# Attention head tiles in three pools, and the first head's three bias tables loaded during the query products

## The chip, the core and the metric

The kernel runs on one core of a Trainium2 chip. The core has a matrix engine (TensorE; PE in the profile, PEld for its weight loads), a vector engine (VectorE, DVE), a scalar engine (ScalarE, ACT), a general engine (GpSimd, POOL) and SyncE, whose queue SP issues all loads and stores of this kernel. Each engine takes its own instructions in order and waits where an operand or a buffer isn't ready. On-chip memory for data is one space in which the kernel opens and closes pools of equal slots; products land in PSUM banks. The metric is the time of one execution in microseconds (us); lower is better.

## What is computed

One layer of a trunk over 1024 latent tokens (a grid of 16 rows of 64) and 256 context tokens, width 1024, all in 32-bit floats:

```python
x = residual(x, swiglu(modnorm(x)))                   # half step
qa, ka, va, ... = project(modnorm(x))                 # one joint projection
o_na  = neighbourhood_attention(qa, ka, va, ...)      # 8 heads of 64
o_mla = blocked_attention(q_mla, k_mla, v_mla)        # 8 latent heads, 96 / 64
x = residual(x, merge(o_na, o_mla, gates))
x = residual(x, swiglu(modnorm(x)))                   # half step

# one grid row of the neighbourhood attention
s_loc = where(valid, q_r @ k_b + rpb[h, row_off, col_off], neg)
s_ctx = q_r @ k_ctx
p = softmax(concat(s_loc, s_ctx))
o = p_loc @ v_b + p_ctx @ v_ctx
```

A neighbourhood query sees a window of 8 by 16 grid cells with a relative bias, and all 256 context keys. Context tokens pass the first half step and the projection only.

## The kernel before

**Stages.** First half step; joint projection; latent, key and value products; query products of the latent attention (`q_heads`); then 64 attention items; merge; second half step. Up to the query products, work is laid out by `Plan`: a list of main steps with side steps spread beside them. Matrix products, turns (transposes on TensorE) and all loads and stores are kept in program order on their engines; the copies of the attention on VectorE and ScalarE may be ordered by the compiler.

**Products.** A 32-bit value is held as a high and a low part, so a product is two or three matrix instructions (`mm3`, `weigh`). All matrix instructions are issued at line 161 (`mmul`), turns at line 164 (`turn_`), loads and stores at line 132 (`put`). In tile names, `bs`, `bm` and `bv` are the three groups of PSUM banks, `w` the head tiles, `xy` tiles of pool y, `xf` of pool f, `t` half tiles, `xu` of pool u, `d` scratch in HBM, `in_bias` the tables.

**Heads and tiles.** A neighbourhood head h (`NaHead.loads`, line 1712) has these tiles, each loaded by SP:

- q and ql (queries, high and low), k (keys of the grid), kvc (context keys, later also context values): 512 KB each for the first three
- three bias tables of 384 KB; column block j uses table `BVAR[j]`, that is 0, 1, 1, 2
- va (values of blocks 0 and 1) and vb (blocks 2 and 3), 512 KB each

Loading is a generator with four steps: q, ql, kvc, k, table 0; table 1 and va; context values into kvc, and vb; table 2. All but table 2 are slots of 4 KB per partition in pool w, which has 13; table 2 lies in pool y with 2 slots. A latent head (`MlaHead`, line 2048) takes six slots of w: qh, ql, kh, kl, v, kvc. A slot may be loaded again once the last reader of the tile in it is done, and SP waits for that in its order.

**Items and rounds.** Item 4h + j of the neighbourhood heads is column block j of head h; items 32 to 63 are the latent heads. Round n of the loop at line 2215 works on the values of item n and starts the scores of item n + 3. A neighbourhood round has three parts (local, context, edge). In each part stand on TensorE, in this order: the turns of this part of item n; half of the scores of item n + 3 (two context and two local products for each half, in the first two parts); and a value product two parts old (`LAG`). So the context product of item n is issued in the first part of round n + 1, and its edge product in the second part. A local score is added to its bias table by VectorE at line 1983, the context score is copied at line 1954, line 1992 takes the exponent.

**When loads are issued.** `ahead_head` (line 2175) issues the first step of head h in the third part of round 4(h-1). `na_item` (line 2136) issues the other steps when item 4h is started, in round 4h - 3. Before the loop, side steps beside the second half of the query products (line 1903) issue three steps of head 0 and the first of head 1, and score items 0 and 1, whose probabilities lie in pool f (`EARLY` = 2). Head 0's table 2 is issued when item 2 is started, in round 0, since pool y opens only after the query products, in memory that pools u and t leave.

**Memory.** On the left side, w (13 slots) and f (2 of 5 KB) lie where pool v was. On the right side, after the query products: o (16), y (2), t (12 of 2 KB), u (10).

Of the kernel before, what the change touches and what calls it, by code (L numbers as in the profile page):

```python
# [8 lines left out]
F32 = mybir.dt.float32  # L9
F32R = mybir.dt.float32r  # L10
# [5 lines left out]
P = 128  # L16
# [22 lines left out]
def f32(ap):  # L39
    return ap.bitcast(F32)  # L40
# [3 lines left out]
def hybrid_block(ctx: ExitStack, tc: tile.TileContext, a: dict, out: bass.AP):  # L44
# [9 lines left out]
    pools = {}  # L54

    def nm(s):
        count[0] += 1
        return f"{s}_{count[0]}"

    def open_pool(key, name, bufs, side):  # L60
        pools[key] = tc.alloc_tile_pool(name=nm(name), bufs=bufs, side=side, reuse_waits="tile")

    def close_pools(*keys):
        for key in keys:
            pools.pop(key).release()

    def U(dt=F32, key="u"):
        return pools[key].tile([P, 1024], dt, tag="u", name=nm("x" + key))
# [1 line left out]
    def V(dt=F32):  # L70
        return U(dt, "v")

    def W(dt=F32R):
        return pools["w"].tile([P, 1024], dt, tag="w", name=nm("w"))

    def T2(dt=F32, n=512):
        return pools["t"].tile([P, n], dt, tag="t", name=nm("t"))
# [34 lines left out]
    class Engine:  # L112


        def __init__(self, e):
            self.e = e
# [5 lines left out]
    def ld(dst, src):  # L122
        for x in [x for x in waiting if x[1].tensor.name == src.tensor.name]:
            waiting.remove(x)
            put(*x[1:])
        return put(dst, src)
# [4 lines left out]
    def put(dst, src):  # L131
        return pin(nc.sync.dma_start(dst, src))
# [987 lines left out]
    class Raw:  # L1120

        us = {(name, hl): [U(F32R, "v") for _ in range(2)] for name in ("a11", "a12") for hl in range(2)}
        f = {}
# [95 lines left out]
    plan = Plan()  # L1219
# [23 lines left out]
    o = len(plan.main)  # L1243
# [64 lines left out]
    o = len(plan.main)  # L1308
# [12 lines left out]
    o, tail = down1.plan(plan)  # L1321
# [110 lines left out]
    def emit_lat(d, ci, x, bank):  # L1432
        t, sq = T2() if bank else x, T2()

        def high():
            if bank:
                act.copy(t, x)
            store(cqT[d][:, ci * 512:(ci + 1) * 512], t)
            act.activation(sq, t, AF.Square)
            later(add, 1)  # L1440

        def add():
            if ci in squares:
                vec.tensor_tensor(squares[ci], squares[ci], sq, op=ALU.add)
            else:
                squares[ci] = sq
        later(high)

    for p in range(3):
        punits.append(Unit(h2, [wc_cols(2 * p), wc_cols(2 * p + 1)],  # L1450
                           lambda i, ci, x, bank, p=p: emit_lat(2 * p + i, ci, x, bank)))
# [21 lines left out]
    o = len(plan.main)  # L1473
# [67 lines left out]
    class Set:  # L1541
# [16 lines left out]
        def loads(self):  # L1558

            return [lambda j=j: self.load(j) for j in range(2)]  # L1560
# [50 lines left out]
    o = len(plan.main)  # L1611
# [97 lines left out]
    class NaHead:  # L1709


        def loads(self, h):
            self.h = h
            i, b = h // 2, (h % 2) * 64
            self.q, self.ql, self.kvc, self.k = q, ql, kvc, k = [W() for _ in range(4)]
            for s in range(2):
                o = 64 * s
                ld(f32(q[o:o + 64, :]), qas[i][0, b:b + 64, :])
                ld(f32(ql[o:o + 64, :]), qas[i][1, b:b + 64, :])
                ld(f32(kvc[o:o + 64, 0:256]), kas[i][s, b:b + 64, NLAT:])  # L1720
            for s in range(2):
                ld(f32(k[64 * s:64 * s + 64, :]), kas[i][s, b:b + 64, :NLAT])
            self.bias = [W(F32)]
            ld(self.bias[0][:, :768], a["bias"][h, 0])
            yield
            self.bias.append(W(F32))
            ld(self.bias[1][:, :768], a["bias"][h, 1])
            self.va = va = W()
            for j in range(2):
                self.values(va, j)  # L1730
            yield
            ld(f32(kvc[:, 256:512]), vcs[h])
            self.vb = vb = W()
            for j in range(2, 4):
                self.values(vb, j)
            yield
            self.bias.append(U(F32, "y"))
            ld(self.bias[2][:, :768], a["bias"][h, 2])
            yield

        def values(self, v, j):
# [3 lines left out]
    def na_loads(h):  # L1745
        heads["na", h] = x = NaHead()
        yield from x.loads(h)
# [97 lines left out]
    o = va_at  # L1845
# [9 lines left out]
    o = len(plan.main)  # L1855
# [4 lines left out]
    o = len(plan.main)  # L1860
# [3 lines left out]
    o = len(plan.main)  # L1864
# [3 lines left out]
    o = len(plan.main)  # L1868
    plan.step(*calls(q_heads(1, cqn[1]), 9))
    heads = {}  # L1870
    EARLY, AHEAD = 2, 3
# [3 lines left out]
    def na_next(h, n=1):  # L1875
        if h not in na_open:
            na_open[h] = na_loads(h)
        for _ in range(n):
            next(na_open[h], None)

    def weights():
        close_pools("v")
        open_pool("w", "weights", 13, "left")
        open_pool("f", "first", EARLY, "left")

    def score_banks():
        banks[0] = "mv"
# [3 lines left out]
    def first_scores(j):  # L1891
        if len(early) == j:
            it = na_item(0, j)
            started.append(it)
            early.append(it.scores())
        next(early[j], None)
# [3 lines left out]
            soft.pop(0)()  # L1900

    plan.spread([weights], o - 4, o - 3)
    plan.spread([lambda h=h: na_next(h) for h in (0, 0, 0, 1)], o - 3, o + 5)
    plan.spread([score_banks], o + 2, o + 3)
    plan.spread([lambda j=j: first_scores(j) for j in (0, 0, 1, 1)], o + 4, o + 8)
    plan.spread([first_soft] * 2, o + 6, o + 9)
# [141 lines left out]
    class MlaHead:  # L2048
        def __init__(self, h):
            self.h = h  # L2050
            self.qh, self.ql, self.kh, self.kl, self.v, self.kvc = [W() for _ in range(6)]
            b, i = (h % 2) * 64, (h % 4) * 32
            for s, x in enumerate((self.qh, self.ql)):
                ld(f32(x[0:64, :]), qns[h // 2][s, b:b + 64, :])
                ld(f32(x[64:QK, :]), qrs[h // 4][s, i:i + 32, :])
                ld(f32(self.kvc[0:64, s * 256:(s + 1) * 256]), kns[h // 2][s, b:b + 64, NLAT:])
                ld(f32(self.kvc[64:QK, s * 256:(s + 1) * 256]), krs[s, :, NLAT:])
            for s, x in enumerate((self.kh, self.kl)):
                ld(f32(x[0:64, :]), kns[h // 2][s, b:b + 64, :NLAT])
                ld(f32(x[64:QK, :]), krs[s, :, :NLAT])  # L2060
            vsv = vs[:, h * P:(h + 1) * P].rearrange("(t p) c -> p t c", p=P)
            ld(f32(self.v).rearrange("p (t c) -> p t c", t=8), vsv[:, 0:8, :])
            ld(f32(self.kvc[:, 512:768]).rearrange("p (t c) -> p t c", t=2), vsv[:, 8:10, :])
# [70 lines left out]
    soft, started = [], []  # L2134
    edges = []
    def na_item(h, j):
        if (j == 0) if h else (j == EARLY):
            na_next(h, 4)
        return NaItem(heads["na", h], j)

# [5 lines left out]
    def items_():  # L2146
        for h in range(NH):
            for j in range(4):
                yield lambda h=h, j=j: na_item(h, j)
        for h in range(NH):  # L2150
            for b in range(4):
                yield lambda h=h, b=b: mla_item(h, b)
# [6 lines left out]

    close_pools("u", "t")  # L2160
    open_pool("o", "heads", 16, "right")
    open_pool("y", "third", 2, "right")
    open_pool("t", "half", 12, "right")
    open_pool("u", "units", 10, "right")
    for x in (ona, omla):
# [9 lines left out]
    def ahead_head(h):  # L2175
        if h < NH:
            na_next(h) if h > 1 else None
        else:
            heads["mla", h - NH] = MlaHead(h - NH)

    def start(n):

        if n < len(todo):
            it = todo[n]()
            started.append(it)
            yield from it.scores()
# [28 lines left out]
    for n in range(len(todo)):  # L2215
        ahead = chain(*[start(x) for x in (range(EARLY, AHEAD + 1) if n == 0 else (n + AHEAD,))])
        for d in range(2):
            if n == len(todo) - 6 + d:
                fm.load(d)
            if n == len(todo) - 5 + d:  # L2220
                fm.split(d)
        parts = started[n].values()
        soft_n, soft[:] = list(soft), []
        for x, part in enumerate(parts):
            pending.append(part())
            for _ in range(-(-len(soft_n) // (len(parts) - x))):
                soft_n.pop(0)()
            for _ in range(5 // len(parts)):
                next(ahead, None)
            if n % 4 == 0 and x == 2 and n // 4 + 1 < 2 * NH:  # L2230
                ahead_head(n // 4 + 1)
            if n >= len(todo) - 3 and (n, x) != (len(todo) - 3, 0) and len(fm.todo) > 4:
                fm.step()
            if len(pending) > LAG:
                pending.pop(0)()
        for _ in ahead:
            pass
    for w in pending:
        w()
        fm.step()  # L2240
# [1 line left out]
        fm.step()  # L2242
    pinned[0] = False

    close_pools("u", "t", "y", "f", "w")
    open_pool("t", "half", TBUFS, "left")
    open_pool("u", "units", 24, "left")

# [35 lines left out]
    plan = Plan()  # L2284
# [5 lines left out]
    for d in range(KD):  # L2290
        o = len(plan.main)
# [21 lines left out]
    plan = Plan()  # L2313
# [30 lines left out]
    o = len(plan.main)  # L2344
# [13 lines left out]
    o = len(plan.main)  # L2358
# [14 lines left out]
    o, tail = down2.plan(plan)  # L2373
# [108 lines left out]
```

## Time and profile before

| | us |
|---|---|
| median of 3 runs | 2557.65 |
| lowest, highest | 2557.51, 2558.33 |
| the profiled execution | 2555.57 |
| its span in the trace | 2553.8 |

Times in the profile are in us from the start of the span. The page lists the busy time of each engine; a view of waits says which engine's instruction ended the idle time of another; a timeline lists instructions in order of time, equal neighbours merged: start, duration, engine, line, operation, output and inputs, shape, count, and in brackets the idle time before it with what ended it. SPq rows are the issue of loads and stores, not their transfer; the time from issue to landing stands in the view of DMA issues. The last columns of the windows' view give the granted clock of TensorE, the busy share of the DMA engines and what they moved in GB/s.

The query products run up to about 1333, the neighbourhood items from there to about 1475, the latent items to about 1742.

### The profile page before, as it was taken

The numbers are of one execution on the slowest core, as the hardware profiler recorded it, in microseconds if no ns is written. First come the engines' busy times: TensorE is split into PE (matmuls) and PEld (weight loads), VectorE is DVE, ScalarE is ACT, GpSimd is POOL, SyncE is SP. The second block draws the span as 40 slices with busy tenths as digits, with TensorE's granted clock in tenths as the row PEclk, the third lists the DMA queues.
The fourth block names the chain that finished last, engine by engine and source line by source line (L and its number), as shares of the span: only waits on it lengthen the run. The fifth ranks groups of instructions, "written<-read, shape, count | busy, mean of one in ns | idle before, by whom it ended". The sixth has DMA issues, their size and how long they took to land.

```text
span 2553.8 us, 38179 instructions
## 1 busy us (share of the span) xinstructions
PE 2526.1 (99%) x13007; PEld 2145.5 (84%) x13007; DVE 1897.7 (74%) x3627; ACT 1249.9 (49%) x2389; POOL 242.5 (9%) x425
## 2 busy tenths in 40 slices
PE   8999999999999999999999999999999999999998
PEld 6888888888888788889889999988888888888887
DVE  5788887898567687874559988886445888777557
ACT  6623223555346753333439888782355322233633
POOL 1000000000002100001007622220030000000001
PEclk9999999999999999999999999999999999999999
DMA  8477765779576665766899832215135667556755
GB/s 315 162 242 236 242 225 189 274 246 297 180 239 221 241 220 190 229 225 200 286 287 243 224 78 77 77 32 210 67 131 179 212 222 236 183 185 251 248 203 193
DMA packets 275475, 523.32 MB, mean 205 GB/s; under 512 B 33424, under 2 KB 84432, under 8 KB 275280
## 3 DMA queue, kind: packets, MB, share of 16 engines
q1 hardware_dynamic: 275280, 520.88, 61.6%
q8 instruction: 103, 1.69, 0.3%
q14 instruction: 92, 0.75, 0.1%
HBM read 375.47 MB, written 145.29 MB: 204 GB/s over the span
## 4 chain that ended last, share of the span: by engine, by line
PE 86%; ACT 6%; DVE 5%; issue 2%; POOL 0%; DMA 0%; DVEq 0%; POOLq 0%; ACTq 0%
PE bs L161 33%; PE bm L161 30%; PE bv L161 20%; ACT xu L2091 2%; PE bm L164 2%; DVE xu L1954 1%; PE bs L164 1%; ACT t L2117 1%; DVE t L2118 1%; DVE xv L120 1%; ACT xu L1992 1%; ACT t L2091 0%; ACT t L1926 0%; ACT t L120 0%; PE bv L164 0%
## 5 line engine op out<-in xcount | busy, mean ns | idle before, releaser
L120 ACT CAST xu<-t 128x512 fp32r<-128x512 f32 x589 | 346.8, 621 | 673.3 <-DVE t L120 558.1
L161 PE MATMUL bm<-xu,xu 128*128 128x512 f32 (+1 forms) x2442 | 596.0, 388 | 0.9 <-ACT t L120 0.9
L161 PEld LDWEIGHTS bm<-xu,xu 128*128 128x128 f32 x2442 | 450.1, 188 | 92.1 <-ACT t L120 2.0
L120 DVE TENSOR_TENSOR xu<-t,xu 128x512 fp32r<-128x512 f32 x589 | 383.0, 688 | 77.5 <-ACT xu L120 77.1
L161 PE MATMUL bs<-xu,xu 128*128 128x512 f32 (+2 forms) x1581 | 388.3, 384 | 0.0
L161 PE MATMUL bs<-xv,xu 128*128 128x512 f32 x1512 | 363.5, 389 | 0.2 <-DVE t L120 0.2
L161 PEld LDWEIGHTS bs<-xu,xu 128*128 128x128 f32 x1581 | 291.7, 188 | 58.0
L161 PE MATMUL bv<-xv,xu 128*128 128x512 f32 x1342 | 336.0, 389 | 0.0
L161 PEld LDWEIGHTS bs<-xv,xu 128*128 128x128 f32 x1512 | 283.5, 188 | 59.7 <-issue 1.0
L161 PEld LDWEIGHTS bv<-xv,xu 128*128 128x128 f32 x1342 | 251.6, 188 | 52.1
L120 DVE TENSOR_TENSOR xu<-xu,xu 128x512 fp32r<-128x512 f32 x282 | 190.0, 689 | 64.4 <-ACT xu L120 63.4
L120 DVE TENSOR_TENSOR t<-t,t 128x512 f32<-128x512 f32 (+4 forms) x350 | 221.2, 635 | 13.5 <-ACT t L120 8.8
L161 PE MATMUL bs<-w,w 96*128 96x512 f32 (+3 forms) x832 | 206.0, 365 | 5.4 <-DVE st L1983 5.4
L161 PE MATMUL bv<-xu,xu 128*128 128x512 f32 x722 | 191.5, 389 | 0.0
L120 POOL TENSOR_SCALAR st<-st 128x1 f32<-128x1 f32 x60 | 27.1, 452 | 1630.9 <-ACT t L120 1283.6
L120 ACT CAST xu<-xu 128x512 fp32r<-128x512 f32 x282 | 169.5, 621 | 11.3 <-DMA xu<-in_f1w 8.0
L161 PEld LDWEIGHTS bv<-xu,xu 128*128 128x128 f32 x722 | 135.5, 188 | 28.1
L161 PE MATMUL bm<-t,xu 128*128 128x256 f32 (+1 forms) x920 | 156.9, 332 | 0.0
L161 PEld LDWEIGHTS bm<-t,xu 128*128 128x128 f32 x920 | 137.4, 189 | 18.6
L161 PE MATMUL bv<-t,w 128*128 128x256 f32 x896 | 150.7, 288 | 1.9 <-DVE t L2118 1.4
L161 PEld LDWEIGHTS bv<-t,w 128*128 128x128 f32 x896 | 133.1, 190 | 17.5 <-DVE t L2118 6.0
L161 PEld LDWEIGHTS bs<-w,w 96*128 96x128 f32 (+1 forms) x832 | 123.2, 190 | 14.2 <-DVE st L1983 7.7
(231 smaller groups left out, 3192.6 us busy)
## 6 DMA issues: line engine op xcount, KB each, us to landing
d<-t SPq DMA_DIRECT2D x432, 256.0 KB, 2.9
t<-d SPq DMA_DIRECT2D x348, 256.0 KB, 5.0
xu<-in_f1w SPq DMA_DIRECT2D x104, 512.0 KB, 4.4
xu<-in_f2w SPq DMA_DIRECT2D x58, 512.0 KB, 4.7
t<-in_wada SPq DMA_DIRECT2D x112, 256.0 KB, 4.5
w<-d SPq DMA_DIRECT2D x112, 256.0 KB, 5.0
t<-in_f1w SPq DMA_DIRECT2D x77, 256.0 KB, 5.0
t<-in_f2w SPq DMA_DIRECT2D x77, 256.0 KB, 5.2
```

The lines of the kernel that those rows point to most:

```text
L120: return lambda *x, **y: pin(f(*x, **y))
L161: return pin(nc.tensor.matmul(o, s, m, start=start, stop=stop, skip_group_check=open_group[0]))
L164: return pin(nc.tensor.transpose(o, x, i))
L1954: nc.vector.tensor_scalar(dst, src, 1.0, FMIN, op0=ALU.mult, op1=ALU.max, accum_out=m)
L1992: soft.append(lambda s=s: nc.scalar.activation(pr[s][:, :640], pr[s][:, :640], AF.Exp, bias=n_[:, s:s + 1], accum_out=l[:, s:s + 1]))
L2091: nc.scalar.activation(x, x, AF.Exp, bias=n_[:, s:s + 1], accum_out=l[:, i:i + 1])
L2117: nc.scalar.copy(t[0], pb)
L2118: nc.vector.tensor_tensor(t[1], pb, f32(t[0]), op=ALU.subtract)
```

## The change

Head tiles are spread over more pools. Pool w falls from 13 slots to 8. The tables go into a pool y of 4 slots of 3 KB per partition, now on the left side and opened with w, before the query products end. For odd neighbourhood heads, kvc and k lie in a new pool p of 2 slots, opened on the right after the query products where y was. Pool f gets a third slot, which no item uses; after round 1 it is closed, and a pool x of 3 slots opens in its place. A latent head takes four slots of w (qh, ql, kh, kl), its kvc from x, and its v from p (the first one's from x).

Beside the query products all four steps of head 0 are now issued, table 2 among them; the first step of head 1 is issued when pool p is open, before the loop.

```diff
-    def W(dt=F32R):
-        return pools["w"].tile([P, 1024], dt, tag="w", name=nm("w"))
+    def W(dt=F32R, key="w", n=1024):
+        return pools[key].tile([P, n], dt, tag=key, name=nm(key))
...
-            self.q, self.ql, self.kvc, self.k = q, ql, kvc, k = [W() for _ in range(4)]
+            self.q, self.ql = q, ql = W(), W()
+            self.kvc, self.k = kvc, k = [W(key="p" if h % 2 else "w") for _ in range(2)]
...
-            self.bias = [W(F32)]
-            ld(self.bias[0][:, :768], a["bias"][h, 0])
-            yield
-            self.bias.append(W(F32))
-            ld(self.bias[1][:, :768], a["bias"][h, 1])
+            self.bias = []
+            for j in range(2):
+                self.bias.append(W(F32, "y", 768))
+                ld(self.bias[j], a["bias"][h, j])
+                if j == 0:
+                    yield
...
-            self.bias.append(U(F32, "y"))
-            ld(self.bias[2][:, :768], a["bias"][h, 2])
+            self.bias.append(W(F32, "y", 768))
+            ld(self.bias[2], a["bias"][h, 2])
...
-        open_pool("w", "weights", 13, "left")
-        open_pool("f", "first", EARLY, "left")
+        open_pool("w", "weights", 8, "left")
+        open_pool("y", "third", 4, "left")
+        open_pool("f", "first", 3, "left")
...
-    plan.spread([lambda h=h: na_next(h) for h in (0, 0, 0, 1)], o - 3, o + 5)
+    plan.spread([lambda: na_next(0)] * 4, o - 3, o + 5)
...
-            self.qh, self.ql, self.kh, self.kl, self.v, self.kvc = [W() for _ in range(6)]
+            self.qh, self.ql, self.kh, self.kl = [W() for _ in range(4)]
+            self.kvc = W(key="x")
...
+            self.v = W(key="p" if h else "x")
...
-        if (j == 0) if h else (j == EARLY):
+        if h and j == 0:
             na_next(h, 4)
...
     open_pool("o", "heads", 16, "right")
-    open_pool("y", "third", 2, "right")
+    open_pool("p", "parts", 2, "right")
+    na_next(1)
...
+        if n == EARLY - 1:
+            close_pools("f")
+            open_pool("x", "parts", 3, "left")
...
-    close_pools("u", "t", "y", "f", "w")
+    close_pools("u", "t", "p", "x", "y", "w")
```

## The prediction

> **What bounds the kernel now.** The page's table of engines comes first: the sum of busy time says how much any change can win.
>
> ```profile
> span 2553.8 us, 38179 instructions
> PE 2526.1 (99%) x13007; PEld 2145.5 (84%) x13007; DVE 1897.7 (74%) x3627; ACT 1249.9 (49%) x2389; POOL 242.5 (9%) x425
> ```
>
> TensorE idles for 2553.8 - 2526.1 = 27.7 us of the whole span. Its list of waits says how much of that lies in the stage that the change touches, the neighbourhood attention:
>
> ```profile
> PE bs L161 <- DVE st L1983: 5.4, 7, 1.9
> ```
>
> Seven waits, 5.4 us, for the instruction that adds the bias table (L1983). The two long ones stand at the start of that stage, in the timeline of TensorE:
>
> ```profile
> 1337.42 1.11 PE L161 MATMUL bs<-w,w 128*128 128x256 f32 x4 [1.39 <-DVE st L1983]
> 1341.92 1.10 PE L161 MATMUL bs<-w,w 128*128 128x256 f32 x4 [1.88 <-DVE st L1983]
> ```
>
> So 1.39 + 1.88 = 3.3 us go there, and about 2.1 us in the other five. That is all the change can win. What it can lose depends on when each head's loads may start, and that is read from the queue SP, which issues every load. Rows of its timeline, in several stretches:
>
> ```profile
> 1334.82 0.32 SPq L132 DMA_DIRECT2D d<-t  x1
> 1335.23 0.41 SPq L132 DMA_DIRECT2D xy<-in_bias  x1
> 1340.83 9.26 SPq L132 DMA_DIRECT2D w<-d  x8
> 1345.17 1.08 SPq L132 DMA_DIRECT2D w<-d  x2
> 1349.00 1.09 SPq L132 DMA_DIRECT2D w<-d  x2
> 1355.12 0.33 SPq L132 DMA_DIRECT2D w<-in_bias  x1
> 1355.97 2.22 SPq L132 DMA_DIRECT2D w<-d  x5
> 1371.69 2.44 SPq L132 DMA_DIRECT2D w<-d  x5
> ```
>
> The eight w<-d at 1340.83 are head 2's q, ql, kvc, k. They stop twice: kvc at 1345.17, k at 1349.00. Each stop ends as another tile of pool w has its last reader:
>
> ```profile
> 1344.57 0.56 DVE L1983 CUSTOM_DVE_ANT_0 xu<-bs,w 128x384 f32<-128x384 f32 x1
> 1345.06 0.08 DVE L1983 DVE_READ_ACCUMULATOR2_ANT st<- 128x1 f32 x1
> ```
>
> ```profile
> 1348.31 0.65 PE L161 MATMUL bv<-xu,w 128*128 128x256 f32 x4
> 1354.45 0.64 PE L161 MATMUL bv<-t,w 128*128 128x256 f32 x4
> 1354.93 0.60 PE L164 MATMUL bm<-ident,xu 128*128 128x128 f32 x4
> 1355.28 0.84 PE L161 MATMUL bs<-w,w 128*128 128x256 f32 x4
> 1355.96 0.64 PE L161 MATMUL bv<-xu,w 128*128 128x256 f32 x4
> 1357.49 0.84 PE L161 MATMUL bs<-w,w 128*128 128x256 f32 x4
> 1371.00 0.84 PE L161 MATMUL bs<-w,w 128*128 128x256 f32 x4
> 1373.39 0.48 PE L161 MATMUL bs<-w,w 128*128 128x256 f32 x2
> ```
>
> kvc goes out at 1345.17, after head 1's first bias table was last read (1345.14); k at 1349.00, after item 1's edge product (1348.96), the last reader of head 0's va; head 2's second table at 1355.12, after item 3's context product (1355.09), the last reader of head 0's kvc. A load takes the slot that comes free next, within 0.05 us, and everything behind it on SP waits too. That queue is the thing to count. Now it keeps ahead: k of head 2 is issued at 1349.00 and first needed by item 8's scores at 1357.49.
>
> **The change, part by part.**
>
> *First head's tables.* Table 2 of head 0 (issued at 1335.23) moves into the query products, and head 1's first step (q, ql, kvc, k, table 0) moves out of them to the front of the attention, since its kvc and k now lie in pool p, opened there. The query products lose 2 MB of loads. TensorE is busy throughout there (columns of the windows' view: stretch, its length, busy time of TensorE and its count, and so on), so I count nothing.
>
> ```profile
> 1310.00:1320.00 10.00, 10.00 (x61) 8.92 (x60) 5.77 (x22) 1.58 (x3) 0.00 (x0) 1.00 1.07 257
> 1320.00:1330.00 10.00, 10.00 (x53) 8.45 (x52) 5.43 (x15) 5.27 (x9) 0.90 (x2) 1.00 0.74 232
> ```
>
> Head 1's nine loads then start at 1335.23, behind the same last store (1334.82). Their pace: the five of 1355.97 take about 0.45 us each, those with the short kvc rows, by the first row below, about 0.62 us.
>
> ```profile
> 1345.66 1.87 SPq L132 DMA_DIRECT2D w<-d  x3
> ```
>
> I take 0.55 us. From issue to landing, asked for loads issued at 1346 to 1347, at 1349.3 to 1350 (an emptier queue), and at 1361.6 to 1362 (a full one):
>
> ```profile
> w<-d SPq DMA_DIRECT2D x2, 256.0 KB, 4.5
> w<-d SPq DMA_DIRECT2D x2, 256.0 KB, 3.9
> w<-d SPq DMA_DIRECT2D x1, 256.0 KB, 7.4
> ```
>
> I take 5.0 us for the last of a batch of seven, with 3.5 and 7.0 as ends; here 5.5, since stores are still in flight. The eighth load, the second half of k, is issued at 1335.23 + 7 x 0.55 = 1339.1 and lands at 1344.6. Item 4's local scores, which read it, begin now some 0.35 us after 1341.92, at 1342.3. **+2.3 us** (0 to 4). The waits of 3.3 us removed before that point buy nothing: TensorE reaches the same missing k earlier.
>
> *Slots of the later heads.* With tables gone, an even head takes 6 slots of w, an odd one 4. Two consecutive heads need 10, and there are 8. For **even heads** (2, 4, 6): when head 2's q, ql, kvc, k are wanted, head 1 holds 4 slots (q, ql, va, vb) until item 7's last scores, and all that head 0 had must be empty but two. q and ql find slots early; kvc must wait for head 0's kvc, that is item 3's context product, ending at 1355.09; k follows with a slot freed by item 7's scores at about 1356.1, which costs nothing more as SP gets there later. The rest of the step stands behind kvc: kvc, q, ql, kvc, k, k, table. The sixth is issued at 1355.09 + 5 x 0.55 = 1357.8 and lands at 1362.8. Item 8's local scores begin now at about 1357.49 + 0.34 = 1357.8. TensorE takes its instructions in order, so the products, turns and later scores queued behind stand too, and with them VectorE and ScalarE. **5.0 us** each (with 0.47 and 3.5: 3.1; with 0.64 and 7.0: 7.5).
>
> For **odd heads** (3, 5, 7): q and ql come from w, kvc and k from p. Head 2 holds 6 slots, head 1 its va and vb: 8, none free. q gets head 1's va after item 5; ql must wait for head 2's q, ql or k, that is item 11's last scores, about 1371.7 (SP's row at 1371.69 now starts on that event), or for head 1's vb, later still. Behind ql stand kvc, q, ql, kvc, k, k: the second k is the seventh, issued at 1371.7 + 6 x 0.55 = 1375.0, landed at 1380.0. Item 12's local scores are due at about 1373.8. **6.2 us** (4.2 to 8.7).
>
> Each wait is measured from an event on TensorE, so one stall does not shorten the next. Three of each: 15.0 + 18.6 = **33.6 us** (21.9 to 48.6). The tables no longer hold SP: with 4 slots in y, each slot was last read before SP comes to it.
>
> *The latent heads.* Their first head needs kl in a slot freed by item 31's last scores, one round before use; kh, kl and kl's second half are issued within some 1.7 us of item 27's context product and land near 6 us after it. The scores that read them come some 4.4 us after it, by the rows of item 3 (1355.09 to item 8's scores at 1357.49, then 2 us of context scores, products and turns). **+1.5 us** (0 to 3). Later ones have longer rounds, 32 of them between the last edge product at 1475.2 and 1741.6, so 8.3 us each, and two whole sets of four slots: nothing.
>
> ```profile
> L161 PE MATMUL bv<-xu,w x128: 276/282/385, 1344.4 to 1475.2; 128*128 128x256 f32 x128
> 1739.38 2.23 PE L161 MATMUL bm<-xo,w 128*128 128x512 f32 x9
> ```
>
> *Pools x and f, and the end.* x opens on memory whose readers ended 26 rounds earlier. At the end the residual branch's loads already wait in the kernel before, and go on waiting for the same two last tiles: nothing, give or take 1 us.
>
> *Gains kept.* The five small waits at the heads' seams, 2.1 us, are covered by the longer ones: **-1.5 us** (-2.1 to 0).
>
> Sum: 2.3 + 33.6 + 1.5 - 1.5 = **+35.9 us**, from +20.3 to +55.6 by the ends. The profiled execution took 2555.57 us (its span and 1.8 us round it), so 2591.5 there; the median of the runs shown is 2557.65, 2.1 us above, so I forecast 2593.5.
>
> **The rivals.**
>
> *Half speed after each stall.* Before its first work TensorE idles for 8.86 us; then the same turns take longer than 4 us later:
>
> ```profile
> 9.52 0.42 PE L164 MATMUL bm<-ident,xv 128*128 128x128 f32 x1
> 11.84 0.42 PE L164 MATMUL bm<-ident,xv 128*128 128x128 f32 x1
> 14.04 0.27 PE L164 MATMUL bm<-ident,xv 128*128 128x128 f32 x1
> ```
>
> They are slow from 8.86 to past 11.84, for some 3.3 us. If a stall of 5 to 6 us brings the same back, at 0.27/0.42 of the pace, each costs 1.2 us more: six of them 7 us, about 2600.5. Against it: the longest idle later is 1.88 us, and no slow turn follows it, so the length from which it decides is not shown. [...]
>
> *The loads arrive in time, and the kernel is faster.* If slots are handed out so that kvc and ql come free a round earlier, or if a whole step lands within the 2.7 us between item 3's context product and item 8's scores, nothing stalls; then the 3.3 us at the start and the 2.1 us at the seams are won: 2557.65 - 5.4 = 2552.2. For it: the fastest load of pool w took 1.9 us. Against it: six loads need 2.8 us for their issue alone, and the count of slots leaves no other order.
>
> ```profile
> DMA to landing us min/median/max: 1.9/4.2/8.8
> ```
>
> *Only the first heads feel it.* SP's blocking could be less than I think if the even heads' kvc found an early slot: then +2.3 us and the seams' gain cancel, 2558. The same time comes out if the change only shuffles idle of the queue.
>
> **How the numbers follow.** Stalls at six heads, full speed: 0.62, at 2593.5. Half speed besides: 0.22, at 2600.5. In time and faster: 0.07, at 2552. No difference: 0.09, at 2558. The first two hold 0.84; their range runs from a little under the low end of the sum (2578) to near its high end (2613): 2575 to 2612, which leaves the other two out. A measurement of this kernel can tell about 0.2%, 5.1 us, from no change. Slower 0.84, faster 0.07, within 0.09.
>
> **What would show it.** Right: from 1340 us on TensorE's bs<-w,w stands idle for 4 to 8 us once a head, ended by a load of w, seven times; SP's w<-d rows of even heads start just after a bv<-t,w product, those of odd heads after the last bs<-w,w; the heads come every 21 to 22 us in place of 15.9 (1357.49 to 1373.39); the query products and the latent heads keep their length; TensorE's idle grows from 27.7 to above 55 us at the same busy time. Wrong: SP's loads of a head issued more than 9 us before its first scores, or stalls ended by L1983 rather than a load.

## The result, and the profile after

| | us |
|---|---|
| before, median of 4 runs | 2557.75 |
| after, median of 4 runs | 2614.69 (2612.52 to 2617.75) |
| ratio | 1.0223, interval 1.0210 to 1.0235 |
| profiled execution, before and after | 2555.57 and 2612.52 |

The change costs 57 us. It was forecast to be slower, by 36 us; the time lies 2.7 us above the range. The table of engines of the changed kernel divides the loss:

```profile
span 2610.7 us, 38181 instructions
PE 2543.0 (97%) x13007; PEld 2161.6 (83%) x13007; DVE 1899.5 (73%) x3627; ACT 1247.7 (48%) x2389; POOL 241.8 (9%) x425
```

TensorE's idle time grew from 27.7 to 2610.7 - 2543.0 = 67.7 us, by 40.0. Its busy time grew too, by 2543.0 - 2526.1 = 16.9 us, for the same 13007 instructions. The two sum to 56.9 us, the whole difference of the profiled executions (56.95).

**The idle part.** The list of waits of TensorE (engine, what it waited for, total us, times, longest) has two new rows, loads of tiles in p and w, and the old row of bias additions (now at line 1986) is down from 5.4 to 1.4 us:

```profile
PE bs L161 <- DMA p<-d: 25.4, 8, 5.6
PE bs L161 <- DMA w<-d: 16.9, 8, 3.7
PE bs L161 <- DVE st L1986: 1.4, 1, 1.4
```

In the timeline of TensorE head 2 looks so:

```profile
1361.13 0.64 PE L161 MATMUL bv<-t,w 128*128 128x256 f32 x4
...
1363.82 0.60 PE L164 MATMUL bm<-ident,xu 128*128 128x128 f32 x4
1367.78 0.48 PE L161 MATMUL bs<-w,w 128*128 128x256 f32 x2 [3.36 <-DMA w<-d]
1369.86 0.98 PE L161 MATMUL bs<-w,w 128*128 128x384 f32 x2 [1.60 <-DMA w<-d]
1370.63 1.05 PE L161 MATMUL bv<-t,p 128*128 128x256 f32 x4
1371.49 1.05 PE L164 MATMUL bm<-ident,xu 128*128 128x128 f32 x4
...
1375.93 0.60 PE L164 MATMUL bm<-ident,xu 128*128 128x128 f32 x4
```

and the same stretch on SP:

```profile
1355.67 0.45 SPq L132 DMA_DIRECT2D w<-d  x1
...
1361.80 1.72 SPq L132 DMA_DIRECT2D w<-d  x3
1362.94 2.50 SPq L132 DMA_DIRECT2D w<-d  x4
```

The last two rows sum up two neighbouring stretches and overlap. The context product of item 3 ends at 1361.77 (1361.13 + 0.64); SP, which has issued nothing since the ql of 1355.67, issues kvc at 1361.80 and then the rest of the step. Item 8's context scores wait 3.36 us for q and kvc, its local scores 1.60 us more for k: 4.96 us. Odd heads, here head 3, wait longer:

```profile
1393.21 0.77 PE L161 MATMUL bs<-p,w 128*128 128x256 f32 x2 [5.34 <-DMA p<-d]
1395.46 0.98 PE L161 MATMUL bs<-p,w 128*128 128x384 f32 x2 [1.48 <-DMA p<-d]
```

**The busy part.** Look at the turns of head 2 above: four take 1.05 us after the wait and 0.60 us from 1375.93 on. The windows' view (the column after POOL's is the granted clock) shows why: TensorE's granted clock is 0.50 there.

```profile
1365.63:1369.04 3.41, 0.48 (x2) 0.31 (x2) 0.37 (x1) 1.20 (x4) 2.52 (x6) 1.00 1.04 217
1369.04:1375.86 6.82, 6.00 (x26) 6.03 (x27) 2.42 (x9) 1.49 (x4) 0.00 (x0) 0.50 0.89 328
1375.86:1379.28 3.42, 3.42 (x29) 3.42 (x29) 3.00 (x10) 3.23 (x8) 2.18 (x4) 1.00 0.00 0
```

The same view puts one window of 20 us round each of the seven waits; the first and the last:

```profile
1340.00:1360.00 20.00, 15.01 (x100) 14.60 (x100) 11.80 (x44) 12.22 (x30) 8.70 (x21) 0.83 0.71 204
...
1485.00:1505.00 20.00, 14.49 (x98) 14.26 (x99) 11.68 (x40) 11.18 (x29) 8.98 (x17) 0.83 0.79 222
```

All seven show a mean clock of 0.83. With a clock of 0.50, as at head 2, the missing 0.17 x 20 = 3.4 us are 6.8 us of half speed each time. Part of it still falls into the wait, and 16.9 / 7 = 2.4 us are lost on work.

### The profile page after: what moved, and what is told of

Its sections match the earlier page's. It is cut to its first block, busy times and chain, and to the rows that moved or that the text cites. A ratio compares the mean times of both kernels' runs of the same rounds, so it can differ in the third digit from the quotient of the medians.

```text
span 2610.7 us, 38181 instructions
## 1 busy us (share of the span) xinstructions
PE 2543.0 (97%) x13007; PEld 2161.6 (83%) x13007; DVE 1899.5 (73%) x3627; ACT 1247.7 (48%) x2389; POOL 241.8 (9%) x425
## 4 chain that ended last, share of the span: by engine, by line
PE 87%; ACT 4%; DVE 3%; DMA 3%; issue 2%; SPq 1%; POOL 0%; DVEq 0%; ACTq 0%; POOLq 0%
PE bs L161 33%; PE bm L161 29%; PE bv L161 21%; PE bm L164 2%; ACT xu L2096 2%; PE bs L164 1%; DVE xu L1957 1%; DMA w<-d 1%; ACT t L2122 1%; DMA p<-d 1%; DVE t L2123 1%; SPq L132 1%; DVE xv L120 1%; PE bv L164 0%; ACT t L2096 0%
## 5 line engine op out<-in xcount | busy, mean ns | idle before, releaser
L161 PE MATMUL bs<-w,w 96*128 96x512 f32 (+2 forms) x512 | 150.5, 405 | 18.3 <-DMA w<-d 16.9
L164 PE MATMUL bm<-ident,xu 128*128 128x128 f32 x836 | 131.3, 277 | 0.0
L2123 DVE TENSOR_TENSOR t<-bm,t 128x512 fp32r<-128x512 f32 x160 | 109.6, 687 | 29.6 <-ACT t L2122 29.0
L1957 DVE TENSOR_SCALAR_CACHE_REDUCE xu<-bs 128x512 f32<-128x512 f32 (+1 forms) x188 | 111.0, 598 | 12.2 <-PE bs L161 11.8
```

Source lines behind the costliest of these rows:

```text
L161: return pin(nc.tensor.matmul(o, s, m, start=start, stop=stop, skip_group_check=open_group[0]))
L164: return pin(nc.tensor.transpose(o, x, i))
L1957: nc.vector.tensor_scalar(dst, src, 1.0, FMIN, op0=ALU.mult, op1=ALU.max, accum_out=m)
L2123: nc.vector.tensor_tensor(t[1], pb, f32(t[0]), op=ALU.subtract)
```

## The experiments

Theory A: a head's loads come late because SP is held by a slot of w that comes free too late (40 us of waits), and each wait of about 5 us is followed by half speed (17 us). The rivals: B, the waits alone, with products slowed by the bunched loads; C, the lost lead of head 1, which the queue never makes up; D and E below.

**Keeping TensorE busy in the waits (e1, e5).** 24 or 40 turns of the unit matrix stand ahead of the first scores of heads 1 to 7.

```diff
                 cs = cx[:, s * 256:(s + 1) * 256]
+                if s + j == 0 and hd.h:
+                    for _ in range(24):
+                        turn_(cs[:, :P], ident, ident)
                 mmul(cs, hd.q[:, o:o + P], hd.kvc[:, 0:256], start=True, stop=False)
```

> The changed kernel, with 24 turns of the unit matrix put on TensorE ahead of the first scores of heads 1 to 7 (their output is overwritten by the scores). About 24 x 0.15 = 3.6 us of work each, in the time in which TensorE waits for a load. Theory A (late loads, and half speed after each wait): the loads land as before, the waits that remain are under 3.5 us, the granted clock of the stage comes back from 0.86 to above 0.97, and some 13 to 17 us of the 57 us are won back: about 2600 us. Rival B (late loads alone; products are slowed by the bunched loads themselves): clock and time as without the turns, 2613 to 2618 us.

Measured: 2606.72 us, 8.0 us less than the changed kernel, with more work on TensorE (ratio to the kernel before 1.0192, 1.0174 to 1.0210, against 1.0210 to 1.0235: a small gain in the times, but a plain one in the trace). Head 2 in the timeline of this run:

```profile
1364.23 2.78 PE L164 MATMUL bs<-ident 128*128 128x128 f32 x24
1368.11 0.48 PE L161 MATMUL bs<-w,w 128*128 128x256 f32 x2 [1.10 <-DMA w<-d]
1370.20 0.60 PE L161 MATMUL bs<-w,w 128*128 128x384 f32 x2 [1.61 <-DMA w<-d]
1371.12 0.60 PE L164 MATMUL bm<-ident,xu 128*128 128x128 f32 x4
```

The load lands where it did, but the products behind it run at full speed (0.60 us for four turns at once; the clock is 1.00 from 1360 to 1376). Rival B falls: the same bunched loads arrive. In odd heads 24 turns, 2.78 us, were too few; each kept a slow stretch, mostly a shorter one (mean clock 0.91 at head 1 over 20 us, 0.93, 0.77 and 0.93 at heads 3, 5 and 7 over 24, 15 and 25 us). Without the turns' 19.5 us TensorE is busy for 2532.7 us here, so 6.6 of the 16.9 us stayed.

> The changed kernel with 40 turns ahead of each head's first scores in place of 24; at the 0.116 us each that 24 of them took, 4.6 us. Theory A: no wait of TensorE is over 2.5 us now, the odd heads' slow stretches go as the even heads' did with 24, the clock of the stage is above 0.97, and the time falls by the rest of the 17 us of slowed work: about 2598 us. Rival B (the loads slow the products in the odd heads): no further gain, 2606 us; or the turns cost more than they save, above 2606 us.

Measured: 2604.14 us, where 2598 was expected, and only 2.6 us less than with 24 turns. Its sums tell why (the turns' group in the view of lines, and the table of engines):

```profile
L164 PE MATMUL bs<-ident 128*128 128x128 f32 x280 | 31.7, 273 | 0.0
```

```profile
span 2602.4 us, 38741 instructions
PE 2561.4 (98%) x13287; PEld 2180.9 (84%) x13287; DVE 1898.5 (73%) x3627; ACT 1248.0 (48%) x2389; POOL 241.9 (9%) x425
```

Without the turns TensorE is busy for 2561.4 - 31.7 = 2529.7 us, 3.6 us above the kernel before in place of 16.9: of the slowed work 13.3 us are gone (heads 3 and 5 keep a slow stretch, mean clocks of 0.86 and 0.89 over 24 and 15 us). But turns and idle are 31.7 + 41.0 = 72.7 us against 67.7 idle before: the turns, 4.5 us a head, outlast the 3.4 us in which even heads wait for kvc. So the slow stretches are shown to come from the idle time, at 2.4 us each; filling it with work wins only part back.

**Slots (e2, e6).** 10 or 9 slots in w, the rest as changed, but for pool f, which goes back to 2 slots with 10. The edit for 10:

```diff
-        open_pool("w", "weights", 8, "left")
+        open_pool("w", "weights", 10, "left")
...
-        open_pool("f", "first", 3, "left")
+        open_pool("f", "first", EARLY, "left")
```

> The changed kernel with 10 slots in w in place of 8 (pool f back to 2 slots to make room); all else as changed. Theory A (slots): two heads then fit, even heads stop waiting; odd heads' k still waits for the other kvc in p, one context product before use, about 2 us each at full clock; head 1 waits as in the changed kernel (5 us and its slow stretch). 2557.7 + 5.5 + 3 x 2 - 1 = about 2568 us. Rival C (the lead that was lost when head 1's first step left the query products is never made up, whatever the slots): all seven waits stay, about 2610 us.

Measured: 2570.28 us, ratio 1.0046 (1.0030 to 1.0062). The wait at head 1 stays, even heads don't wait for loads, head 5 waits for k in p as expected (heads 3 and 7 wait 2.5 and 2.4 us at the same instruction, which the view puts down to VectorE):

```profile
1346.40 0.98 PE L161 MATMUL bs<-p,w 128*128 128x384 f32 x2 [1.64 <-DMA p<-d]
1414.51 0.60 PE L161 MATMUL bs<-p,w 128*128 128x384 f32 x2 [2.07 <-DMA p<-d]
```

Rival C falls: with slots, the queue makes up its lead at once.

> The changed kernel with 9 slots in w. Theory A by the count of slots: q, ql and kvc of even heads find slots early, only k waits for item 3's context product (about 2 us, full clock); odd heads as with 8 slots (7 us and a slow stretch of 2.4 us), head 1 too. 2557.7 + 5.5 + 3 x 2 + 3 x 9.2 - 1 = about 2596 us. Rival E (the number of free slots acts smoothly, half way between 8 and 10): odd heads gain as well, 2592 us or less, with odd waits near 4.5 us.

Measured: 2576.62 us, 20 us better than expected. Even heads wait 1.9 to 2.2 us for k, as expected, but odd heads lose their long waits as well:

```profile
1366.80 0.60 PE L161 MATMUL bs<-w,w 128*128 128x384 f32 x2 [1.95 <-DMA w<-d]
1421.95 0.59 PE L161 MATMUL bs<-p,w 128*128 128x384 f32 x2 [2.70 <-DMA p<-d]
```

Neither the odd waits of 7 us that A expected came, nor those of 4.5 us of rival E. E falls by the run before: the odd heads wait 1.9 to 2.7 us here and 2.1 to 2.5 us with 10 slots, so the tenth slot gives them nothing. For A, the count was wrong, not the rule. When head 3 asks for q and ql, head 2 holds 6 slots and head 1 only vb, since va was read out with item 5: with 9 slots two are free, with 8 one. So an odd head lacks exactly one slot in the changed kernel. SP's rows agree: there ql of head 3 goes out at 1386.11, behind item 11's scores; in this run it went out at 1374.9, behind item 5's edge product. One slot of 4 KB is worth 2614.69 - 2576.62 = 38 us.

**Head 1's lead alone (e3).** The kernel before, with head 1's first step behind the query products.

```diff
-    plan.spread([lambda h=h: na_next(h) for h in (0, 0, 0, 1)], o - 3, o + 5)
+    plan.spread([lambda: na_next(0)] * 3 + [lambda: None], o - 3, o + 5)
...
     open_pool("y", "third", 2, "right")
+    na_next(0)
+    na_next(1)
```

> The kernel before, with one edit: head 1's first step is issued after the query products, behind head 0's third table, as in the changed kernel; pools as before (13 slots). Theory A: one wait of about 5 us at item 4 and a slow stretch of 2.4 us after it, less the 1.9 us wait that stood there: about 2563 us, later heads as before. Rival C (lost lead never made up): waits at every head, 2590 us or more.

Measured: 2562.26 us against 2558.33 of the kernel before, run beside it, ratio 1.0014 (1.0004 to 1.0023). One pair of waits, at item 4, and none for loads after it:

```profile
1345.72 0.48 PE L161 MATMUL bs<-w,w 128*128 128x256 f32 x2 [3.43 <-DMA w<-d]
1347.82 0.98 PE L161 MATMUL bs<-w,w 128*128 128x384 f32 x2 [1.62 <-DMA w<-d]
```

**What stands behind the held load (e4).** The first step's loads by tile, not by half.

```diff
             for s in range(2):
                 o = 64 * s
                 ld(f32(q[o:o + 64, :]), qas[i][0, b:b + 64, :])
-                ld(f32(ql[o:o + 64, :]), qas[i][1, b:b + 64, :])
-                ld(f32(kvc[o:o + 64, 0:256]), kas[i][s, b:b + 64, NLAT:])
+            for s in range(2):
+                ld(f32(ql[64 * s:64 * s + 64, :]), qas[i][1, b:b + 64, :])
+            for s in range(2):
+                ld(f32(kvc[64 * s:64 * s + 64, 0:256]), kas[i][s, b:b + 64, NLAT:])
```

> The changed kernel, with the first step's loads in the order q, q, ql, ql, kvc, kvc, k, k in place of q, ql, kvc, q, ql, kvc, k, k. Theory A (what stands on SP behind the blocked load is late by its place): for even heads four loads go out ahead of the blocked kvc and k is the fourth behind it, not the sixth: 1.1 to 1.6 us less at each; for odd heads one load less behind the blocked ql: 0.5 us. Waits fall by about 5 us, time to about 2609 us. Rival D (the transfers, not their issue, set the landing: same bytes, same end): no change.

Measured: 2600.87 us, 13.8 us less (10.2 by the profiled executions); the direction of A, about twice its size, and rival D, no change, falls. Even heads now wait 2.4 to 2.6 us for loads and 0.4 us for VectorE (before 5.0), odd ones 5.3 to 5.6 (before 6.5 to 7.2):

```profile
1411.27 0.60 PE L161 MATMUL bs<-w,w 128*128 128x384 f32 x2 [2.46 <-DMA w<-d]
1431.94 0.55 PE L161 MATMUL bs<-p,w 128*128 128x256 f32 x2 [3.82 <-DMA p<-d]
1433.97 0.98 PE L161 MATMUL bs<-p,w 128*128 128x384 f32 x2 [1.48 <-DMA p<-d]
```

From the issue of the held load to the local scores it takes 5.9 to 6.0 us in even heads (8.1 to 8.3 in the changed kernel) and 7.6 to 8.0 us in odd ones (9.0 to 9.7). Two 256 KB loads fewer behind the held one are thus worth 2.2 us on average in even heads, one fewer 1.6 us in odd ones: 1.1 to 1.6 us a load, not the 0.55 us of its issue. What makes up the rest was not shown.

**What the change set out to do (e7, e8, e9).** All loads of head 0 and the first step of head 1 beside the query products, 10 slots in w; only k of the later heads in p, since its slot is free a round before it is wanted. e7:

```diff
-            self.kvc, self.k = kvc, k = [W(key="p" if h % 2 else "w") for _ in range(2)]
+            self.kvc, self.k = kvc, k = W(), W(key="p" if h > 1 else "w")
...
-    plan.spread([lambda: na_next(0)] * 4, o - 3, o + 5)
+    plan.spread([lambda h=h: na_next(h) for h in (0, 0, 0, 0, 1)], o - 3, o + 5)
...
-            self.v = W(key="p" if h else "x")
+            self.v = W(key="p")
...
-            open_pool("x", "parts", 3, "left")
+            open_pool("x", "parts", 2, "left")
```

> What the change set out to do, without the lost lead: 10 slots in w, tables in 4 slots of y, f of 2 slots; only k of the heads from 2 on lies in p, since its slot is free a whole round before it is wanted again; all four steps of head 0 and the first of head 1 go out beside the query products. A latent head has v in p, kvc in x. Theory A: no wait for a load in heads 1 to 7, about 1 us at the first latent head; of the kernel before's 5.4 us of waits those at the start (1.9 us) and the seams (2 us) may go: 2553 to 2558 us. Rival C (bunching at the start costs a wait whatever the slots): 2560 us or more.

Measured: 2583.94 us, a miss. The time would fit rival C, which here says that bunched loads cost a wait at the start; but the waits don't stand there. The waits, and two places of the timeline:

```profile
PE bs L161 <- DMA w<-d: 14.8, 9, 3.4
PE bs L161 <- DMA x<-d: 2.9, 5, 0.9
```

```profile
1359.91 0.48 PE L161 MATMUL bs<-w,w 128*128 128x256 f32 x2 [3.40 <-DMA w<-d]
1361.99 0.98 PE L161 MATMUL bs<-p,w 128*128 128x384 f32 x2 [1.59 <-DMA p<-d]
...
1562.04 0.70 PE L161 MATMUL bs<-w,w 96*128 96x512 f32 x2 [2.23 <-DMA w<-d]
```

I had made the changed kernel's mistake twice over. Head 1, with k in w, leaves head 2's kvc the slot of head 0's kvc again; and the latent heads' kvc, with 2 slots, must wait for the kvc of two heads earlier, read to the end of its last item, while kh and kl stand behind it on SP. Against e7, e8 gives kvc a third slot (p with 3, v in x with 2), head 2's kvc one in p, and y only 3 slots to make room.

```diff
-            self.kvc, self.k = kvc, k = W(), W(key="p" if h > 1 else "w")
+            self.kvc, self.k = kvc, k = W(key="p" if h == 2 else "w"), W(key="p" if h > 1 else "w")
+            if h == 1:
+                yield
             self.bias = []
...
-            self.v = W(key="p")
+            self.v = W(key="x")
...
-            self.kvc = W(key="x")
+            self.kvc = W(key="p")
```

> As the run before with all loads early, with the two late slots mended: p has 3 slots (k of heads from 2 on, kvc of head 2, and later the latent heads' kvc), x has 2 for the latent heads' v, y has 3 slots, and head 1's first table is issued with its second. Theory A (a tile with 2 slots is late when its last reader is the head's last context product, as kvc is; with 3, or for k and v, it is not): no wait for a load in heads 1 to 7, at most 1 us in the latent heads, busy time of TensorE back to 2526 us: 2553 to 2558 us. Rival C (loads bunched beside the query products or at the start cost something by themselves): 2560 us or more, with the loss ahead of 1340 us.

Measured: 2562.02 us against 2559.07, ratio 1.0012 (1.0003 to 1.0021), above the 2553 to 2558 expected. The waits of the latent heads are gone; the longest left is at item 4, for head 1's first table, which the extra `yield` moves behind the products, and head 2 still waits for k, which A did not expect:

```profile
1349.22 1.49 PE L161 MATMUL bs<-w,w 128*128 128x256 f32 x4 [3.23 <-DVE st L1988]
1364.29 0.59 PE L161 MATMUL bs<-p,w 128*128 128x384 f32 x2 [1.73 <-DMA p<-d]
```

e9 takes that `yield` out again.

> As the run before with three slots, but head 1's first table is again issued with its first step, beside the query products; with 3 slots in y it has to wait on SP for item 0's second half of scores. Theory A: the 3.2 us wait at item 4 goes (it was for that table), the 1.4 us before it and about 1.7 us at head 2 stay: 2557 to 2560 us, no difference from the kernel before that can be measured. Rival C: held stores or bunched loads cost as much as the wait: 2561 us or more.

Measured: 2555.81 us against 2558.44, ratio 0.9992 (0.9983 to 1.0001): no difference from the kernel before that can be told. TensorE is busy for 2525.7 us of a span of 2552.9, and no wait for a head's tile is over 0.6 us. So fetching everything beside the products does no harm, and this form of rival C falls too; what it can win is within the noise. One row of its waits tells why:

```profile
PE bs L161 <- DVE st L1986: 4.2, 5, 1.4
```

With the loads in time, 4.2 of the 5.4 us of waits for the bias addition are still there, and VectorE's own list of waits has no load between 1333 and 1480. The wait of 1.39 us at the first items stands in every run. So most of the 5.4 us that the change was to win at best were no waits for tables.

## Why the prediction was right and wrong

| term, us | forecast | measured in the trace |
|---|---|---|
| head 1 | +2.3 | 4.98 + 1.39 - 3.27 = +3.1 |
| heads 2, 4, 6 | 3 x 5.0 | 4.96, 5.05, 4.95 |
| heads 3, 5, 7 | 3 x 6.2 | 6.82, 7.17, 6.47 |
| latent heads | +1.5 (the first) | 1.16 (the first) + 0.77 (the third) = +1.9 |
| seams | -1.5 | -2.1 |
| other idle time | 0 | +1.7 |
| slower work behind the waits | 0 | +16.9 |
| sum | 35.9 | 56.9 |

The bound, the place and the cause of the waits held; that TensorE would idle more "at the same busy time" did not, and the heads come every 24 us, not 21 to 22. Of the other idle time 1.3 us lie ahead of 929 us, at the start of the kernel (a first wait of 9.34 us in place of 8.86) and near 860 to 870 us, where the change does nothing; from there to item 0's first scores, now at 1333.70, both kernels take 404.7 us, so the query products kept their length. SP issues head 2's kvc 0.03 us after item 3's context product, as the count of slots had it, and the local scores start 8.1 us after that product where 7.75 was forecast. That the gain at the start cannot be kept held too: e3 shows that head 1's late step by itself costs more than the wait that it replaces. But the first of the two waits there, 1.39 us, was counted as removed and stayed.

The step that failed is the choice between the forecast and the rival "half speed after each stall". I gave the rival 0.22 and priced it at 1.2 us a stall, 7 us in all for six; it happened at all seven waits and cost 2.4 us each. Two things were mis-sized. Whether a wait in mid-kernel brings it was read as open, since the longest idle stretch behind the start was 1.88 us; all seven waits, of 4.95 to 7.17 us, brought it. And the price was scaled from the start of the kernel, 3.3 us at 0.27/0.42 of the pace; here a slow stretch of work lasts from 1369.86 to about 1375.9, 6 us, at 0.60/1.05 and a granted clock of 0.50. With 16.9 us in the sum the forecast would have been 2610, inside the range. The upper end of the range, 2612, was that of a sum without this term. (The low end of that sum, given as +20.3, adds up to 21.9 - 2.1 = 19.8; nothing hangs on it.)

The smaller error lies in the odd heads, 6.2 against 6.8 on average; in e4 a load in a batch cost 1.1 to 1.6 us, more than the 0.55 us taken for its issue. In the count, "its va and vb" should have been vb alone for head 1 at that point; with 8 slots the answer is the same, q early and ql late, so the forecast did not suffer, but the expectation for 9 slots did.

## What to carry to other kernels

Count slots by the last reader of each tile, at the moment when the next head's first load wants one, and look at what stands behind that load on a queue that keeps its order, as SP's here (nothing issued from ql at 1355.67 to kvc at 1361.80): one slot of 4 KB missing cost 38 us here. In this kernel a tile that is read to the end of a head, as kvc is, needs a third slot (e7 against e8); one that is read out a round earlier, as k is, does with two (e7: at most 0.7 us from head 3 on). Waits of TensorE like these, 4.95 to 7.17 us, should be priced with the half-speed stretch behind them: here 16.9 us on 40.4 us of waits at the seven heads, four tenths more.

## What the runs showed of the hardware

Waits of about one length were followed by half speed in one place and not in another. Head 4 in the run with the loads in another order (e4) and head 7 in the run with 10 slots (e2) have a single wait, of 2.46 and of 2.40 us; the granted clock behind it is 0.50 for 3.41 us:

```profile
1408.61:1412.02 3.41, 0.95 (x7) 0.79 (x6) 0.92 (x2) 1.74 (x4) 3.08 (x6) 1.00 1.00 286
1412.02:1415.43 3.41, 3.41 (x17) 3.41 (x16) 2.20 (x8) 0.59 (x1) 0.00 (x0) 0.50 1.05 388
```

```profile
1445.05:1448.46 3.41, 1.08 (x10) 0.88 (x8) 3.29 (x11) 2.89 (x9) 2.21 (x5) 1.00 0.86 249
1448.46:1451.87 3.41, 3.33 (x14) 3.37 (x15) 0.78 (x4) 1.33 (x3) 2.13 (x5) 0.50 1.04 381
```

But a longer wait of the same run with 10 slots, 2.52 us at head 3, left the clock at 1.00:

```profile
1376.78:1380.19 3.41, 2.05 (x18) 1.84 (x16) 3.32 (x12) 2.98 (x8) 2.14 (x5) 1.00 0.85 202
1380.19:1383.60 3.41, 2.25 (x17) 2.28 (x18) 2.12 (x8) 2.32 (x5) 3.03 (x6) 1.00 1.03 357
1383.60:1387.02 3.42, 3.42 (x30) 3.42 (x29) 3.14 (x10) 2.79 (x8) 1.26 (x4) 1.00 1.07 355
```

In the changed kernel, where the waits at a head sum to 4.95 to 7.17 us, the clock is 0.50 for 6.82 us at head 2, and for as long at the other six heads by their mean of 0.83 over 20 us.

The wait of 1.39 us at the first items, which all runs have, came with half speed in one run (e2, 1.40 us there, the first two rows) and not in the kernel before (the last two):

```profile
1335.82:1339.23 3.41, 2.02 (x11) 1.38 (x10) 3.33 (x13) 2.58 (x6) 0.26 (x1) 1.00 0.97 276
1339.23:1342.64 3.41, 2.88 (x13) 2.38 (x11) 2.11 (x11) 0.49 (x2) 1.60 (x7) 0.50 1.03 204
...
1334.22:1337.64 3.42, 2.03 (x13) 1.52 (x12) 3.34 (x10) 2.46 (x6) 0.00 (x0) 1.00 0.79 237
1337.64:1341.05 3.41, 2.40 (x16) 1.95 (x15) 1.84 (x10) 1.40 (x4) 1.87 (x7) 1.00 0.95 324
```

What decides whether half speed follows a wait was not shown.
